# A hybrid HGRN2 and Conformer step on one core: norms whose intermediate values stand in PSUM, and a squared ReLU made by ACT in its PSUM bank

## The chip, the cores and the metric

The kernel runs on one core of a Trainium2 chip. The metric is the device time of one execution in microseconds. TensorE is called PE (its weight loads PEld), VectorE DVE, ScalarE ACT, GpSimd POOL and SyncE SP, as in the profile.

## What is computed

Two layers work on 640 tokens of 1024 features in float32: 128 context tokens and 512 latent tokens. Each layer has a mixer (layer 0 a bidirectional gated linear recurrence, layer 1 a convolution module) and a squared-ReLU MLP with 4096 hidden features. Ahead of each stands an RMS norm with a scale and a shift, which differ between context and latent tokens; the convolution module has a layer norm of its own, and a final norm ends the step. Cut to what matters here:

```python
y = xf * lax.rsqrt(jnp.mean(xf * xf, axis=-1, keepdims=True) + EPS)
hp = rmsnorm(xp, norm_mlp[i]) * (1.0 + m_ctx[4]) + m_ctx[3]
hs = rmsnorm(xs, norm_mlp[i]) * (1.0 + m_lat[4]) + m_lat[3]
return jnp.square(jax.nn.relu(h @ w1)) @ w2
# conformer_conv, after the depthwise convolution
uf = (uf - mu) * lax.rsqrt(var + EPS) * ln_g + ln_b
return jax.nn.silu(uf) @ w_pw2
```

## The kernel before, in words

**Layout and matmuls.** Features lie on the 128 partitions in eight tiles (k = 0 to 7), tokens on the free axis. Tokens go in two halves, A (tag "a", "c") and B ("b", "d"), of 320 and 320 columns, or in layer 1 after the convolution of 304 and 336 (COLS, L52). A half A holds context and latent columns, so that `segs` (L55) cuts it in two segments, 128 and 192 (or 176) columns; a half B is one segment. Each float32 operand is split in a rounded part `hi` and a rest `lo` (both fp32r): `split` (L168) has ACT copy the source to `hi` (L169) and DVE subtract it (L170). A unit of `linear` (L210) is one output tile of 128 features: eight k by three matmuls (L180, L183, L184), 24 in all, summed in one of the three PSUM banks of pool `mmp`, and then an evacuation function that is handed the bank.

**Weights.** `fetch` (L154) keeps three units ahead: a DMA to `rw`, ACT's rounding to `wh` (L161), and the rest `wl` (L165) made by DVE or, in a large part of the program (up to about 1300 us), by POOL in four pieces of 128x256.

**The order of the work.** The program is written as one stream. Background steps stand in the list `bg` with a cost each; after every unit `between` (L195) lets as many run as the budget pays for, and `drain` (L204) runs the rest. A scheduler in the framework then sorts each engine's instructions by the order of the program and its own estimate of when they are ready, hands out the buffers of each pool in turn, and adds the waits. Each engine then runs its own list strictly in order.

**Norms.** `rms_stat` (L246) squares each tile on ACT (to `nsq`, SBUF, L256) and sums on DVE (to `nacc`, L257). `inv_rms` (L226) has two forms. The usual one sums over partitions with a matmul of `ones` (ps_n, L230), takes the root on ACT into the SBUF tile `rs` (L232), and has DVE invert it in place (L233). The by-token form (the two norms ahead of layer 0's MLP, and half B of the final norm) works on a few columns (L238 to L240) and spreads the result by matmuls into the PSUM tile ps_n (L242). `norm_steps` (L272) then applies it tile by tile: DVE multiplies x by rs into `nt` (SBUF, two buffers, L278); `modulate` (L264) scales and shifts `nt` in place, segment by segment, on DVE for the four k in `on_dve` (L270) and on ACT for the others (L268); `split` makes hi and lo.

**The layer norm of the convolution.** The taps (L794) sum in two PSUM banks at a time of pool `scp` (three banks); `mean` (L815) sums with a matmul of `ones` (ps_mu, L817) and has ACT copy it, divided by D, to the SBUF tile `mu` (L819); `sub` (L822) subtracts it from the eight tiles of `yc`; then come `rms_stat`, a multiplication by rs (L828), ACT's Silu (L829), all in place in `yc`, and `split`.

**Hidden units of the MLP.** `hid_evac` (L699) takes a unit's bank `ps`: ACT makes the ReLU into the SBUF tile `hr` (L703), DVE multiplies it by ps (L704), which is the bank's last use, and `split` makes hi and lo of `hr`. There are 128 such units. The units of `mlp_out` and of the mixers' output projections are evacuated by `residual` (L284), one DVE instruction per segment (L287).

**Where the norms stand.** After the output projection of layer 0 the norms of both halves (L733), with the loads and DVE sums (L128, `scratch`) for layer 1's scales behind them; half A's norm of layer 1 (L842) beside `mlp_in` of B; the layer norm of half A and the norm of half B (L849 to L856) beside `pw2` and `pw1`; the layer norm of half B (ahead of L862); the norm ahead of half B's last MLP (L863); the final norm (L872).

Of the kernel before, what the change touches and what calls it, by code (L numbers as in the profile page):

```python
# [48 lines left out]
ND = (1, 3, 5, 7)  # L49
ND0 = (0, 2, 4, 6)  # L50
# [19 lines left out]
def hybrid_step(ctx: ExitStack, tc: tile.TileContext, xt, vec, pos, masks, ident_in, state, c_rows, w_mod0, w_modt,  # L70
# [18 lines left out]
    pool.memset(ones[:], 1.0)  # L89
    eps = const.tile([P, 2], F32, name="eps")  # L90
# [135 lines left out]
    def inv_rms(tp, acc, n, by_token):  # L226

        ps = axp.tile([P, 512], F32, tag="ax", name="ps_n")
        if not by_token:
            pe.matmul(ps[:, :n], ones[:], acc, start=True, stop=True)  # L230
            rs = tp.tile([P, HW], F32, tag="rs", name="rs")
            act.activation(rs[:, :n], ps[:, :n], AF.Sqrt, bias=eps[:, 0:1], scale=1.0 / D)  # L232
            dve.reciprocal(rs[:, :n], rs[:, :n])  # L233
            return rs[:, :n]
# [11 lines left out]
    def rms_stat(tp, xs, n, by_token=False):  # L246
# [3 lines left out]
        def sq(k):  # L250
# [3 lines left out]
            else:  # L254
                t = tp.tile([P, HW], F32, tag="nsq", name="nsq", bufs=2)
                act.activation(t[:, :n], xs(k), AF.Square)  # L256
                dve.tensor_tensor(box["acc"][:, :n], box["acc"][:, :n], t[:, :n], ALU.add)  # L257
# [6 lines left out]
    def modulate(t, layer, which, k, lo, hi, eng=act):  # L264
        for s, a, b in segs(lo, hi):
            r, sc, bi = t[:, a - lo:b - lo], amod[:, layer, which, k, s:s + 1], mvec(layer, 3 * which, k, s)
            if eng is act:
                act.activation(r, r, AF.Identity, bias=bi, scale=sc)  # L268
            else:
                eng.tensor_scalar(r, r, sc, bi, ALU.mult, ALU.add)  # L270

    def norm_steps(tp, x, layer, which, acts, lo, hi, by_token, on_dve):  # L272
# [3 lines left out]
        def apply(k):  # L276
            t = tp.tile([P, HW], F32, tag="nt", name="nt", bufs=2)
            dve.tensor_tensor(t[:, :n], x[:, k, lo:hi], box["rs"], ALU.mult)  # L278
            modulate(t, layer, which, k, lo, hi, dve if k in on_dve else act)
            split(t[:, :n], acts[k][0][:, :n], acts[k][1][:, :n])  # L280
# [26 lines left out]
    with tc.tile_pool(name="start", bufs=1) as st:  # L307
# [78 lines left out]
        def first_norm(k0, k1):  # L386
            for k in range(k0, k1):
                pin(dve.tensor_tensor(x0[:, k], x0[:, k], rs[:], ALU.mult), int(k > 4))
                modulate(x0[:, k], 0, 0, k, 0, NT, dve)
# [306 lines left out]
    rp = ctx.enter_context(tc.tile_pool(name="rp", bufs=2))  # L696


    def hid_evac(hid):  # L699
        def evac(u, half, lo, hi, ps):  # L700
            n = hi - lo
            r = rp.tile([P, HW], F32, tag="hr", name="hr")
            act.activation(r[:, :n], ps, AF.Relu)  # L703
            dve.tensor_tensor(r[:, :n], ps, r[:, :n], ALU.mult)  # L704
            split(r[:, :n], hid[half][u][0][:, :n], hid[half][u][1][:, :n])
# [12 lines left out]

    def start_norm(layer, which, half, cols, first=True, by_token=False, on_dve=ND):

# [248 lines left out]
```

## Time and profile before

| | |
|---|---|
| median of three runs | 1619.97 us (1619.37 to 1620.06) |
| the profiled execution, its own time | 1616.84 us |
| its span, first to last instruction | 1614.9 us |
| mean granted clock of PE | 0.989 |
| busy: PE, DVE, ACT, POOL | 98%, 77%, 47%, 43% |

The span is 1.9 us short of the execution's own time, and this execution is 3.1 us under the median. PE's clock column gives the granted clock as a share of 2.4 GHz; 0.5 is 1.2 GHz. A wait is an engine's idle time ahead of an instruction, put down to the instruction that came last. A matmul's duration is longer than the distance to the next one, since matmuls are pipelined: 172 of them with 320 columns start in 25 us, one every 145 ns.

### The profile page before, as it was taken

Reading aid. Unit: us, or ns where it says so; the run is one execution under the profiler, and the core shown is the slowest. Engines: PE = TensorE matmul, PEld = TensorE weight load, DVE = VectorE, ACT = ScalarE, POOL = GpSimd, SP = SyncE. Lnnn points to the kernel's source line nnn. Section 1 sums busy time; section 2 is a strip of 40 time slices with the busy share of each in tenths; the row PEclk is TensorE's granted clock in tenths of the full one; section 3 lists DMA queues with packets and bytes.
Section 4 is the critical chain, followed back from the end, with each engine's and each line's share of the span. In section 5 each row is a group of like instructions: output and inputs, shape, how many; then the busy total and the mean of one; then the engine's idle time right before and its main releaser. Section 6 shows DMA issues by size and latency. Waiting matters only on the chain.

```text
span 1614.9 us, 32111 instructions
## 1 busy us (share of the span) xinstructions
PE 1578.3 (98%) x12810; PEld 1536.0 (95%) x12810; DVE 1249.4 (77%) x2222; ACT 761.9 (47%) x1227; POOL 694.0 (43%) x863
## 2 busy tenths in 40 slices
PE   8999999999999999999999999999999899999997
PEld 6899999988899999999999999989999899999997
DVE  5788888878738998788789997899999686555544
ACT  3566666665446313344454334764344554334321
POOL 3100000000484765555978888789898710000000
PEclk7999999999999999999999999999999999999998
DMA  9333333333253556766544444345454344444401
GB/s 360 129 112 113 112 112 113 112 109 103 101 190 122 181 183 224 235 225 208 169 144 144 156 146 145 129 134 169 157 164 148 122 153 158 144 144 144 144 27 66
DMA packets 71302, 240.11 MB, mean 149 GB/s; under 512 B 7792, under 2 KB 14576, under 8 KB 70128
## 3 DMA queue, kind: packets, MB, share of 16 engines
q1 hardware_dynamic: 71152, 238.06, 44.4%
q8 instruction: 101, 1.65, 0.4%
q14 instruction: 49, 0.40, 0.1%
HBM read 234.36 MB, written 3.67 MB: 147 GB/s over the span
## 4 chain that ended last, share of the span: by engine, by line
PE 76%; DVE 17%; POOL 2%; ACT 2%; issue 2%; DMA 0%; SPq 0%; DVEq 0%; POOLq 0%; ACTq 0%
PE ps_mm L180 23%; PE ps_mm L184 22%; PE ps_mm L183 22%; DVE ps_cv L794 3%; POOL wl L165 2%; DVE scratch L128 2%; PE ps_sc L504 2%; DVE nt L278 1%; DVE nacc L257 1%; DVE cl L170 1%; PE ps_u L588 1%; DVE hr L704 1%; DVE nt L270 1%; DVE yc L822 1%; DVE al L170 1%
## 5 line engine op out<-in xcount | busy, mean ns | idle before, releaser
L165 POOL TENSOR_TENSOR wl<-rw,wh 128x256 fp32r<-128x256 f32 x808 | 668.8, 861 | 568.1 <-ACT wh L161 561.6
L161 ACT CAST wh<-rw 128x1024 fp32r<-128x1024 f32 x334 | 348.4, 1046 | 314.4 <-PE ps_mm L184 230.8
L180 PE MATMUL ps_mm<-bh,wh 128*128 128x320 f32 (+1 forms) x1000 | 317.8, 318 | 2.8 <-ACT nt L268 2.6
L180 PE MATMUL ps_mm<-ah,wh 128*128 128x320 f32 (+1 forms) x1000 | 311.6, 312 | 1.9 <-ACT ah L169 1.1
L183 PE MATMUL ps_mm<-bh,wl 128*128 128x320 f32 (+1 forms) x1000 | 311.4, 312 | 0.0
L184 PE MATMUL ps_mm<-bl,wh 128*128 128x320 f32 (+1 forms) x1000 | 310.8, 311 | 0.0
L184 PE MATMUL ps_mm<-al,wh 128*128 128x320 f32 (+1 forms) x1000 | 308.0, 308 | 1.7 <-DVE al L170 1.7
L183 PE MATMUL ps_mm<-ah,wl 128*128 128x320 f32 (+1 forms) x1000 | 308.0, 308 | 0.0
L794 DVE SCALAR_TENSOR_TENSOR ps_cv<-ub,vt,ps_cv 128x319 f32<-128x319 f32 (+1 forms) x464 | 228.7, 555 | 0.4
L165 DVE TENSOR_TENSOR wl<-rw,wh 128x1024 fp32r<-128x1024 f32 x132 | 168.7, 1280 | 39.6 <-ACT wh L161 39.6
L180 PEld LDWEIGHTS ps_mm<-ah,wh 128*128 128x128 f32 x1000 | 188.6, 189 | 7.3 <-issue 3.4
L180 PEld LDWEIGHTS ps_mm<-bh,wh 128*128 128x128 f32 x1000 | 188.0, 188 | 5.7 <-ACT nt L268 2.8
L183 PEld LDWEIGHTS ps_mm<-ah,wl 128*128 128x128 f32 x1000 | 188.5, 188 | 3.2 <-issue 2.6
L184 PEld LDWEIGHTS ps_mm<-al,wh 128*128 128x128 f32 x1000 | 188.6, 189 | 3.1 <-DVE al L170 2.2
L183 PEld LDWEIGHTS ps_mm<-bh,wl 128*128 128x128 f32 x1000 | 187.9, 188 | 0.5
L184 PEld LDWEIGHTS ps_mm<-bl,wh 128*128 128x128 f32 x1000 | 188.1, 188 | 0.1
L287 DVE SCALAR_TENSOR_TENSOR xr<-ps_mm,mod,xr 128x128 f32<-128x128 f32 (+2 forms) x240 | 97.8, 434 | 112.3 <-PE ps_mm L184 111.9
L180 PE MATMUL ps_mm<-ch,wh 128*128 128x320 f32 (+1 forms) x576 | 176.8, 307 | 4.4 <-ACT ch L169 2.3
L180 PE MATMUL ps_mm<-dh,wh 128*128 128x320 f32 (+1 forms) x576 | 180.7, 314 | 0.0
L184 PE MATMUL ps_mm<-dl,wh 128*128 128x320 f32 (+1 forms) x576 | 180.0, 313 | 0.0
L183 PE MATMUL ps_mm<-dh,wl 128*128 128x320 f32 (+1 forms) x576 | 179.7, 312 | 0.0
L184 PE MATMUL ps_mm<-cl,wh 128*128 128x320 f32 (+1 forms) x576 | 176.7, 307 | 1.8 <-DVE cl L170 1.8
(209 smaller groups left out, 2550.4 us busy)
## 6 DMA issues: line engine op xcount, KB each, us to landing
rw<-in_w_mlp SPq DMA_DIRECT2D x230, 512.0 KB, 3.4
wm<-in_w_modt SPq DMA_DIRECT2D x80, 512.0 KB, 4.2
rw<-in_w_pw SPq DMA_DIRECT2D x48, 512.0 KB, 3.3
rw<-in_w_in SPq DMA_DIRECT2D x40, 512.0 KB, 3.5
wmb<-in_w_mod SPq DMA_DIRECT2D x8, 1024.0 KB, 10.1
rw<-in_w_out SPq DMA_DIRECT2D x16, 512.0 KB, 3.4
x<-in_xt SPq DMA_DIRECT2D x8, 320.0 KB, 5.7
xr<-in_xt SPq DMA_DIRECT2D x8, 320.0 KB, 6.2
```

The costliest lines, as they stand in the source:

```text
L128: tc.keep_in_program_order(dve.scalar_tensor_tensor(scratch, box["w"][:], 1.0, cbs[:, s], ALU.mult, ALU.mult, accum_out=raw_m[:, i, s:s + 1]))
L161: act.copy(wh[:], rw[:])
L165: eng.tensor_tensor(wl[:, k:k + step], rw[:, k:k + step], wh[:, k:k + step].bitcast(F32), ALU.subtract)
L170: eng.tensor_tensor(lo, src, hi.bitcast(F32), ALU.subtract)
L180: first = pe.matmul(ps[:, :n], wh[:, k, :], hi[:, :n], start=k == 0, stop=False)
L183: pe.matmul(ps[:, :n], wl[:, k, :], hi[:, :n], start=False, stop=False)
L184: pe.matmul(ps[:, :n], wh[:, k, :], lo[:, :n], start=False, stop=k == KT - 1)
L257: dve.tensor_tensor(box["acc"][:, :n], box["acc"][:, :n], t[:, :n], ALU.add)
L270: eng.tensor_scalar(r, r, sc, bi, ALU.mult, ALU.add)
L287: dve.scalar_tensor_tensor(x[:, u, a:b], ps[:, a - lo:b - lo], mvec(layer, chunk, u, s), x[:, u, a:b], ALU.mult, ALU.add)
L504: pe.matmul(ps[r:r + w, t * w:(t + 1) * w], x[:, s0:s0 + w], y[:, t0:t0 + w], start=True, stop=True, tile_position=(0, r))
L794: dve.scalar_tensor_tensor(box[i][:, :m], u[:, j:j + m], w, box[i][:, :m], ALU.mult, ALU.add)
```

## The change

The norms' helper tiles move from SBUF to PSUM. `nsq`, `nt` and the layer norm's `lt` take banks of pool `scp` (three banks in turn); the root and its inverse are made in place in the bank ps_n, and the mean stays in ps_mu (the division by D moves into a second constant matrix `ones_d`). In `norm_steps` one DVE instruction per segment multiplies x by the scale and by rs; ACT adds the shift on its way to hi; a second DVE instruction adds the shift again and subtracts hi to give lo. In `hid_evac` ACT makes ReLU and square in place in the unit's bank, and `split` reads the bank. The pool `rp`, the tiles `rs`, `nt`, `nsq`, `mu` in SBUF and the choice `on_dve` go away. By instructions per tile: half A before, one DVE multiplication, one hi, one lo, and two segment instructions on DVE or ACT; after, four on DVE and two on ACT, of half the width on average. Half B before, DVE two or three and ACT two or one; after, DVE two and ACT one. Per hidden unit: before, DVE two and ACT two; after, DVE one and ACT three.

```diff
--- before.py
+++ after.py
@@ -46,8 +46,6 @@
 CUT = 304
 CA = 5
 TM0 = True
-ND = (1, 3, 5, 7)
-ND0 = (0, 2, 4, 6)
 CB = 6
 COLS = (((0, HALF), (HALF, NT)), ((0, CUT), (CUT, NT)))
 
@@ -87,6 +85,8 @@
     mask = const.tile([P, NMASK, SB], U8, name="mask")
     ones = const.tile([P, P], F32, name="ones")
     pool.memset(ones[:], 1.0)
+    ones_d = const.tile([P, P], F32, name="ones_d")
+    pool.memset(ones_d[:], 1.0 / D)
     eps = const.tile([P, 2], F32, name="eps")
     pool.memset(eps[:, 0:1], EPS)
     pool.memset(eps[:, 1:2], EPS * P)
@@ -228,10 +228,9 @@
         ps = axp.tile([P, 512], F32, tag="ax", name="ps_n")
         if not by_token:
             pe.matmul(ps[:, :n], ones[:], acc, start=True, stop=True)
-            rs = tp.tile([P, HW], F32, tag="rs", name="rs")
-            act.activation(rs[:, :n], ps[:, :n], AF.Sqrt, bias=eps[:, 0:1], scale=1.0 / D)
-            dve.reciprocal(rs[:, :n], rs[:, :n])
-            return rs[:, :n]
+            act.activation(ps[:, :n], ps[:, :n], AF.Sqrt, bias=eps[:, 0:1], scale=1.0 / D)
+            dve.reciprocal(ps[:, :n], ps[:, :n])
+            return ps[:, :n]
         c = n // 4
         rc = tp.tile([P, 4], F32, tag="rc", name="rc", bufs=2)
         for i in range(4):
@@ -252,32 +251,34 @@
                 box["acc"] = tp.tile([P, HW], F32, tag="nacc", name="nacc", bufs=2)
                 act.activation(box["acc"][:, :n], xs(0), AF.Square)
             else:
-                t = tp.tile([P, HW], F32, tag="nsq", name="nsq", bufs=2)
+                t = scp.tile([P, 512], F32, tag="sc", name="nsq")
                 act.activation(t[:, :n], xs(k), AF.Square)
-                dve.tensor_tensor(box["acc"][:, :n], box["acc"][:, :n], t[:, :n], ALU.add)
+                dve.tensor_tensor(box["acc"][:, :n], t[:, :n], box["acc"][:, :n], ALU.add)
 
         def fin():
             box["rs"] = inv_rms(tp, box["acc"][:, :n], n, by_token)
 
         return box, [(0.45, lambda k=k: sq(k)) for k in range(KT)] + [(0.3 if by_token else 2.1, fin)]
 
-    def modulate(t, layer, which, k, lo, hi, eng=act):
+    def modulate(t, layer, which, k, lo, hi):
         for s, a, b in segs(lo, hi):
             r, sc, bi = t[:, a - lo:b - lo], amod[:, layer, which, k, s:s + 1], mvec(layer, 3 * which, k, s)
-            if eng is act:
-                act.activation(r, r, AF.Identity, bias=bi, scale=sc)
-            else:
-                eng.tensor_scalar(r, r, sc, bi, ALU.mult, ALU.add)
-
-    def norm_steps(tp, x, layer, which, acts, lo, hi, by_token, on_dve):
+            dve.tensor_scalar(r, r, sc, bi, ALU.mult, ALU.add)
+
+    def norm_steps(tp, x, layer, which, acts, lo, hi, by_token):
         n = hi - lo
         box, steps = rms_stat(tp, lambda k: x[:, k, lo:hi], n, by_token)
 
         def apply(k):
-            t = tp.tile([P, HW], F32, tag="nt", name="nt", bufs=2)
-            dve.tensor_tensor(t[:, :n], x[:, k, lo:hi], box["rs"], ALU.mult)
-            modulate(t, layer, which, k, lo, hi, dve if k in on_dve else act)
-            split(t[:, :n], acts[k][0][:, :n], acts[k][1][:, :n])
+            t = scp.tile([P, 512], F32, tag="sc", name="nt")
+            for s, a, b in segs(lo, hi):
+                c = slice(a - lo, b - lo)
+                sh = mvec(layer, 3 * which, k, s)
+                dve.scalar_tensor_tensor(t[:, c], x[:, k, a:b], amod[:, layer, which, k, s:s + 1], box["rs"][:, c],
+                                         ALU.mult, ALU.mult)
+                act.activation(acts[k][0][:, c], t[:, c], AF.Identity, bias=sh)
+                dve.scalar_tensor_tensor(acts[k][1][:, c], t[:, c], sh, acts[k][0][:, c].bitcast(F32),
+                                         ALU.add, ALU.subtract)
 
         return steps + [(0.85, lambda k=k: apply(k)) for k in range(KT)]
 
@@ -386,7 +387,7 @@
         def first_norm(k0, k1):
             for k in range(k0, k1):
                 pin(dve.tensor_tensor(x0[:, k], x0[:, k], rs[:], ALU.mult), int(k > 4))
-                modulate(x0[:, k], 0, 0, k, 0, NT, dve)
+                modulate(x0[:, k], 0, 0, k, 0, NT)
                 for half, (lo, hi) in enumerate(COLS[0]):
                     split(x0[:, k, lo:hi], h[half][k][0][:, :HALF], h[half][k][1][:, :HALF], (dve, pool)[half])
 
@@ -693,16 +694,14 @@
 
     linear(4, h, g_last, both, 4, lambda: None, 4)
     oright.close()
-    rp = ctx.enter_context(tc.tile_pool(name="rp", bufs=2))
 
 
     def hid_evac(hid):
         def evac(u, half, lo, hi, ps):
             n = hi - lo
-            r = rp.tile([P, HW], F32, tag="hr", name="hr")
-            act.activation(r[:, :n], ps, AF.Relu)
-            dve.tensor_tensor(r[:, :n], ps, r[:, :n], ALU.mult)
-            split(r[:, :n], hid[half][u][0][:, :n], hid[half][u][1][:, :n])
+            act.activation(ps, ps, AF.Relu)
+            act.activation(ps, ps, AF.Square)
+            split(ps, hid[half][u][0][:, :n], hid[half][u][1][:, :n])
         return evac
 
     hid = {}
@@ -716,10 +715,10 @@
     def mlp_out(layer, cols, group=8, done=None):
         linear(8, hid, residual(xr, layer, 5), cols, group, done=done)
 
-    def start_norm(layer, which, half, cols, first=True, by_token=False, on_dve=ND):
+    def start_norm(layer, which, half, cols, first=True, by_token=False):
 
         h[half] = new_act("ab"[half])
-        steps = norm_steps(tp, xr, layer, which, h[half], *cols, by_token, on_dve)
+        steps = norm_steps(tp, xr, layer, which, h[half], *cols, by_token)
         bg[:] = steps + bg if first else bg + steps
         return steps[-1]
 
@@ -730,7 +729,7 @@
 
     budget[1] = 3.0
     for cols in (A0, B0):
-        linear(8, on, residual(xr, 0, 2), cols, done=lambda half: start_norm(0, 1, half, COLS[0][half], False, TM0, ND0))
+        linear(8, on, residual(xr, 0, 2), cols, done=lambda half: start_norm(0, 1, half, COLS[0][half], False, TM0))
     drain()
     with tc.tile_pool(name="wm1", bufs=1) as wmp:
         scratch = wmp.tile([P, D], F32, name="scratch")
@@ -814,9 +813,8 @@
 
         def mean():
             ps = axp.tile([P, 512], F32, tag="ax", name="ps_mu")
-            pe.matmul(ps[:, :n], ones[:], lnb["sum"][:, :n], start=True, stop=True)
-            lnb["mu"] = cv.tile([P, HW], F32, tag="mu", name="mu")
-            act.activation(lnb["mu"][:, :n], ps[:, :n], AF.Copy, scale=1.0 / D)
+            pe.matmul(ps[:, :n], ones_d[:], lnb["sum"][:, :n], start=True, stop=True)
+            lnb["mu"] = ps
 
         def sub(k):
             dve.tensor_tensor(lnb["y"][:, k, :n], lnb["y"][:, k, :n], lnb["mu"][:, :n], ALU.subtract)
@@ -824,8 +822,9 @@
         box, steps = rms_stat(tp, lambda k: lnb["y"][:, k, :n], n)
 
         def fin(k):
-            y = lnb["y"][:, k, :n]
-            dve.tensor_tensor(y, y, box["rs"], ALU.mult)
+            t = scp.tile([P, 512], F32, tag="sc", name="lt")
+            y = t[:, :n]
+            dve.tensor_tensor(y, lnb["y"][:, k, :n], box["rs"], ALU.mult)
             act.activation(y, y, AF.Silu, bias=v("ln_b")[:, k:k + 1], scale=v("ln_g")[:, k:k + 1])
             split(y, acts[k][0][:, :n], acts[k][1][:, :n])
 
```

## Rows read from the trace of the kernel before

**Rows 1.** The page's first part: busy time, share of the span, instructions of each engine.

```profile
PE 1578.3 (98%) x12810; PEld 1536.0 (95%) x12810; DVE 1249.4 (77%) x2222; ACT 761.9 (47%) x1227; POOL 694.0 (43%) x863
```

**Rows 2.** Waits of PE: total us, times, longest us.

```profile
PE ps_n L238 <- DVE nacc L257: 4.4, 2, 2.6
...
PE ps_n L230 <- DVE nacc L257: 2.8, 2, 1.7
PE ps_mm L180 <- ACT nt L268: 2.6, 1, 2.6
PE ps_mm L180 <- ACT ch L169: 2.3, 1, 2.3
...
PE ps_mm L180 <- DVE xr L287: 2.1, 2, 1.3
...
PE ps_mm L184 <- DVE cl L170: 1.8, 5, 0.9
PE ps_mm L184 <- DVE al L170: 1.7, 2, 1.2
PE ps_mm L180 <- ACT ah L169: 1.1, 1, 1.1
```

**Rows 3.** Windows of 25 us: busy us (instructions) by engine, PEclk, DMA share, GB/s.

```profile
500.00:525.00 25.00, 22.43 (x149) 22.16 (x148) 18.97 (x42) 14.12 (x29) 9.76 (x12) 0.93 0.32 106
...
800.00:825.00 25.00, 22.25 (x138) 21.26 (x137) 22.05 (x37) 17.38 (x33) 17.25 (x23) 0.93 0.38 126
825.00:850.00 25.00, 25.00 (x173) 25.00 (x172) 22.24 (x50) 9.22 (x15) 22.88 (x33) 1.00 0.49 159
...
1050.00:1075.00 25.00, 21.56 (x144) 20.77 (x144) 21.62 (x39) 18.63 (x28) 22.66 (x29) 1.00 0.45 149
```

**Rows 4.** DVE lines from 400 to 1300 us: min/median/max ns.

```profile
L257 DVE TENSOR_TENSOR nacc<-nacc,nsq x51: 466/758/7968, 451.3 to 1300.0; 128x320 f32<-128x320 f32 x28, 128x304 f32<-128x304 f32 x14, 128x336 f32<-128x336 f32 x9
...
L278 DVE TENSOR_TENSOR nt<-xr,rs x24: 465/624/1024, 804.1 to 1087.0; 128x320 f32<-128x320 f32 x16, 128x304 f32<-128x304 f32 x8
...
L822 DVE TENSOR_TENSOR yc<-yc,mu x16: 460/1006/1048, 1000.2 to 1252.9; 128x304 f32<-128x304 f32 x8, 128x336 f32<-128x336 f32 x8
...
L170 DVE TENSOR_TENSOR dl<-hr,dh x32: 493/748/1043, 529.4 to 997.1; 128x320 fp32r<-128x320 f32 x32
...
L704 DVE TENSOR_TENSOR hr<-ps_mm,hr x88: 460/480/494, 508.5 to 1253.8; 128x320 f32<-128x320 f32 x64, 128x304 f32<-128x304 f32 x24
```

**Rows 5.** The same line of DVE after 1300 us, where POOL has no work.

```profile
L170 DVE TENSOR_TENSOR dl<-hr,dh x32: 500/501/502, 1343.4 to 1548.9; 128x336 fp32r<-128x336 f32 x32
```

**Rows 6.** DVE groups by shape: busy us, mean ns, idle before.

```profile
L287 DVE SCALAR_TENSOR_TENSOR xr<-ps_mm,mod,xr 128x128 f32<-128x128 f32 x80 | 27.8, 347 | 53.0 <-PE ps_mm L184 52.9
...
L287 DVE SCALAR_TENSOR_TENSOR xr<-ps_mm,mod,xr 128x192 f32<-128x192 f32 x40 | 16.3, 407 | 0.0
...
L287 DVE SCALAR_TENSOR_TENSOR xr<-ps_mm,mod,xr 128x320 f32<-128x320 f32 x40 | 21.8, 544 | 11.9 <-PE ps_mm L184 11.7
...
L270 DVE TENSOR_SCALAR nt<-nt,amod,mod 128x320 f32<-128x320 f32 x8 | 4.5, 560 | 0.0
...
L233 DVE RECIPROCAL rs<-rs 128x320 f32<-128x320 f32 x2 | 4.3, 2146 | 3.7 <-ACT rs L232 3.7
```

**Rows 7.** ACT groups by shape: busy us, mean ns, idle before.

```profile
L703 ACT ACTIVATE hr<-ps_mm 128x320 f32<-128x320 f32 x64 | 27.9, 436 | 86.0 <-PE ps_mm L184 86.0
...
L161 ACT CAST wh<-rw 128x1024 fp32r<-128x1024 f32 x334 | 348.4, 1046 | 314.4 <-PE ps_mm L184 230.8 <-POOL wl L165 69.2 <-DMA rw<-in_w_pw 5.4
```

**Rows 8.** Timeline of DVE around 1250 us, then ACT: start us, us.

```profile
1249.98 3.91 DVE L822 TENSOR_TENSOR yc<-yc,mu 128x336 f32<-128x336 f32 x4
...
1253.81 0.46 DVE L704 TENSOR_TENSOR hr<-ps_mm,hr 128x304 f32<-128x304 f32 x1
...
1254.31 0.45 ACT L169 CAST ch<-hr 128x304 fp32r<-128x304 f32 x1 [3.25 <-DVE hr L704]
```

**Rows 9.** Timeline at the end of the program, PE.

```profile
1604.82 0.76 PE L238 MATMUL ps_n<-ones,nacc 128*84 128x1 f32 x8 [1.78 <-DVE nacc L257]
```

## The prediction

> **What bounds the kernel now.** I read the page's busy times first: PE is busy for 1578.3 us of the span of 1614.9 [rows 1], so what can be won is the 36.6 us in which it idles, and what a low clock takes from it. Nothing in the change touches a unit's 24 matmuls. The waits of PE come next [rows 2]: almost all that are over a microsecond stand at norms, and they end on DVE (the sum nacc, the residual xr, the rest al or cl) or on an ACT step that itself stood behind DVE (nt, ch). The windows show how large the holes are: a full stretch starts 173 matmuls in 25 us, the stretch of layer 1's first norm 138, and there the granted clock is 0.93 on average [rows 3]. So has the stretch of layer 0's norms [rows 3]. A clock that is at 2.4 GHz or at 1.2 was then at 1.2 for 0.07 x 25 / 0.5 = 3.5 us, which costs at most 1.75 us beside the waits themselves.
>
> Why DVE is late is seen in its own lines. Instructions with both inputs in SBUF have medians of 624 to 1006 ns while POOL makes weight rests, and maxima over 1000; the one that reads a PSUM bank beside the same POOL work has 480, and never over 494 [rows 4]. After 1300 us, where POOL rests, the slow line costs 501 [rows 5]. So a PSUM operand takes DVE out of POOL's way. The change gives nearly every DVE instruction of the norms one PSUM operand, and that is the main term.
>
> **The change, part by part.** The two-input forms that are new (multiply by scale and rs; add the shift, subtract hi) are nearest to the residual, which has one PSUM and one SBUF tensor and a scalar: 347, 407 and 544 ns for 128, 192 and 320 columns [rows 6]. A sum, subtraction or multiplication with a PSUM operand I price at 0.48, the hi-lo subtraction of a hidden unit too. As far ends I keep 0.46, the fastest of these lines, and 1.05, the slowest [rows 4], by which nothing would be won.
>
> *A tile of a norm* costs DVE before 0.62 (multiply), 0.28 (half of the tiles modulated at 0.56, taken as one piece) and 0.75 (lo, as for a hidden unit): 1.65 [rows 4, 6]. After, a half A has two segments: 2 x (0.347 + 0.407) = 1.51. A half B: 2 x 0.544 = 1.09. A sum of squares goes from 0.76 to 0.48, a mean's subtraction from 1.01 to 0.48, a hidden unit from 0.48 + 0.75 to 0.48. What this is worth is read place by place, never more than the wait there:
>
> 1. Norms of layer 0's MLP. Wait 2.6 (of the 4.4 on L238 the other 1.8 is the final norm [rows 2, 9]), with up to 1.75 of low clock. Their rs is in PSUM already, so a tile of half A goes from 1.51 to 1.51; seven sums save 7 x 0.28 = 1.9. I take 1.8 of 4.3.
> 2. Layer 1's first norm, half A. Waits on al and ah 1.7 + 1.1, low clock 1.75: 4.5; the window agrees, 35 matmuls short at 145 ns, 5.1 [rows 2, 3]. DVE saves 8 x 0.14 + 5 hidden units x 0.75 = 4.8. PE wants tile 7 only 21 x 0.145 = 3.0 us after tile 0 and DVE needs 1.5 us a tile, so a remnant stays: 3.5.
> 3. Layer norm, half A: wait 1.7 on L230. Eight subtractions and seven sums save 4.2 + 1.9, and the copy of the mean goes: all 1.7.
> 4. Norms beside pw1 of half B: 2.6 on nt and 0.8 on xr. DVE saves 8 x (1.65 - 1.09) + 6 x 0.28 = 6.2, but the next norm's sums compete: 2.9 of 3.4 (the window is 29 matmuls short, 4.2, with the room that the norm's own matmul takes [rows 3]).
> 5. Layer norm, half B: ch 2.3, cl 0.9, nacc 1.1 (2.8 less 1.7). The timeline shows the cause: four subtractions hold DVE for 3.91 us, the squared ReLU's multiplication stands behind them, and hi waits 3.25 us for it [rows 8]. After, hi needs ACT alone. The chain from the last subtraction to the sum stays: 3.0 of 4.3.
> 6. Layer 0's MLP beside the scale loads: xr 1.3 and four small waits on cl, 0.9. DVE stays full of those loads' sums: 1.4 of 2.2.
>
> Sum 14.3; all the waits together 20.4. The end of the program (1.8 us on nacc [rows 9]) keeps its chain residual, square, sum, and POOL rests there: nothing. The extra constant of the mean is one POOL memset behind the one that PE waits for: nothing.
>
> *What is added.* ACT makes 128 more squares of about 0.436 us [rows 7], 56 us in a program in which it is busy for 762 [rows 1]; the idle 53% hides them; its part of a norm's tile stays at one or two instructions. A bank is held for ReLU, square, hi and lo, 3 x 0.44 + 0.48 = 1.8, with one weight rounding of 1.05 between them 2.9, where before it was 0.9; PE wants that bank again two units later, 2 x 24 x 0.145 = 7.0, so 4.1 us cover it. At a change from mlp_in to mlp_out in one half (12 places) the cover is thinner: hi of the last tile is ready 3 x 0.44 + 1.05 = 2.4 after the unit, and PE wants it at 3.05. A second rounding in between makes it 3.45, 0.4 late: up to 4.8 us in all, in the range and not in the sum. Behind the waiting ACT stands the next rounding, whose weights are wanted three units later.
>
> *The reciprocal in PSUM* is shown by no row of this trace. From SBUF it takes 2.15 for 320 columns [rows 6]. At the other end it takes double, and four of them (places 2 to 5) lie ahead of a wait: 8.6. Below, it could gain only the hundredths by which PSUM and undisturbed SBUF differ. I take 2.15: at 6.7 ns a column it is nearly four times slower than the multiply-add from SBUF at 1.75, so it isn't the reading that bounds it. The Trainium skill, VectorE: DVE Perf Modes, section Why PSUM operands drop a tier, says that an instruction with a PSUM operand can't use both SBUF read ports, and that fp32 then runs at its single rate. By that rule the double price is the one to fear, and the sum would be 14.3 - 8.6 = 5.7.
>
> The profiled execution takes 1616.84, its span and 1.9 around it; 14.3 less is 1602.5. It lies 3.1 under the median of the runs, so against that median, 1619.97, the forecast is 1605.7. A difference of 0.2% (3.2 us) is what a measurement of this kernel can tell.
>
> **The rivals.**
> *Partly given back.* The phase changes cost their 4.8, or one or two reciprocals their double: 9 us stay, 1611. For it: ACT's list is strictly in order. Against: ACT is idle for long stretches.
> *DVE and ACT take turns at a bank.* In a half A the second segment's multiplication goes to the bank that ACT reads for the first, and each lo waits for its hi. If DVE waited each of these out, a tile would take 1.51 + 2 x 0.44 = 2.4, 0.75 more than the 1.65. Places 1 and 2 turn to +6.0 - 1.9 = 4.1 and +6.0 - 3.7 = 2.3 lost, the other four keep 9.0: 2.6 won, 1617.4, no change that can be told. Against: three banks in turn let other tiles fill the gaps. The Trainium skill, PSUM — Partial Sum Buffer, section PSUM bank collisions raise a hardware error, says that two engines may not be in one bank and quadrant at once, reads included. By it the turns are forced, and only the filling is open.
> *PE's own list* (slower). The sum's matmul stands at a fixed place in PE's list, set from estimates when the program is built, and blocks every unit behind it. Two of the three largest entries of [rows 2] are that. If the estimates for the new forms are too short, each of ten such matmuls (two by token, six norms, two means) waits like the worst now, 2.6: 26 in place of 5.4, while places 2, 4, 6 and the ch of 5 still win 9.8: 10.8 slower, 1630.8. It decides from 1.5 us per matmul on. Against: DVE's work ahead of each sum gets shorter whatever the list says.
> *Nothing arrives.* The waits move to other instructions of the same places: 1619.
>
> **How the numbers follow.** Forecast 0.58, partly given back 0.20, turns 0.08, nothing arrives 0.05, PE's list 0.09. Faster 0.78, within 0.2% 0.13, slower 0.09. The time is the likeliest case's, 1605.7. The range runs from all waits gone, 1619.97 - 20.4 = 1599.6, to the turns at 1617.4; it leaves out the slower case, the empty one and a little at the ends.
>
> **What would show it.** Right: the sums, subtractions and multiplications of the norms near 0.48 us also beside POOL; DVE's busy time down by 75 us or more (128 x 0.6 for the hidden units alone); full windows at the norms; PE's waits on nt, ch, ah and xr under 2 us together. Wrong: a reciprocal of 4 us; PE waits on ps_n or ps_mu longer than now; new waits on hi or lo at the changes from mlp_in to mlp_out; or DVE idle behind ACT inside a norm of half A.

## The result and the profile after

The changed kernel takes 1594.13 us (median of four runs, 1593.40 to 1595.34) beside 1619.67 for the kernel before on the same chip (four runs, 1618.63 to 1620.06): ratio 0.9845 [0.9833, 0.9857], 25.5 us or 1.6% faster. Forecast were 1605.7 and a range from 1599.6: the sign was right and the gain nearly twice as large as forecast, 5.5 us beyond the near end of the range.

The profiled execution after takes 1594.12 us, its span 1592.3. First its page, busy time and chain of work:

```profile
PE 1572.4 (99%) x12810; PEld 1532.4 (96%) x12810; DVE 1127.9 (71%) x2106; ACT 797.9 (50%) x1341; POOL 662.3 (42%) x864
...
PE 87%; DVE 5%; POOL 2%; ACT 2%; issue 2%; DMA 1%; SPq 0%; DVEq 0%; POOLq 0%; ACTq 0%
```

Against [rows 1] PE idles for 19.9 us in place of 36.6, DVE works 121.5 us less, and ACT only 36 more. The waits of PE after (total us, times, longest us):

```profile
PE ps_s L372 <- DVE acc L334: 3.3, 1, 3.3
PE ps_rb L683 <- DVE o_all L685: 2.2, 2, 1.2
PE ps_n L237 <- DVE nacc L256: 1.7, 1, 1.7
...
PE ps_mm L180 <- ACT ah L279: 1.3, 2, 0.8
...
PE ps_mm L184 <- DVE bl L280: 0.9, 1, 0.9
```

Of the norms' waits [rows 2] 1.3 on ah, 0.9 on bl and the 1.7 at the end of the program [rows 9] are left. The two largest entries belong to layer 0's recurrence and to its output heads, which the change doesn't touch. DVE's lines from 400 to 1300 us (min/median/max ns), the same work as in [rows 4]:

```profile
L256 DVE TENSOR_TENSOR nacc<-nsq,nacc x56: 464/492/509, 450.5 to 1291.8; 128x320 f32<-128x320 f32 x28, 128x304 f32<-128x304 f32 x14, 128x336 f32<-128x336 f32 x14
...
L820 DVE TENSOR_TENSOR yc<-yc,ps_mu x16: 464/484/504, 990.0 to 1231.4; 128x304 f32<-128x304 f32 x8, 128x336 f32<-128x336 f32 x8
...
L827 DVE TENSOR_TENSOR lt<-yc,ps_n x16: 466/488/511, 1005.9 to 1252.2; 128x304 f32<-128x304 f32 x8, 128x336 f32<-128x336 f32 x8
...
L170 DVE TENSOR_TENSOR dl<-ps_mm,dh x32: 473/492/494, 524.7 to 988.2; 128x320 fp32r<-128x320 f32 x32
```

Medians of 748 to 1006 ns and maxima over 1000 (once 7968) have become 484 to 492 with no instruction over 511, beside a POOL that does the same work as before (808 subtractions). The layer norm's multiplication `lt`, not among [rows 4], had a median of 880 and a maximum of 1046. By shape (busy us, mean ns, idle before) the new forms stand so:

```profile
L277 DVE SCALAR_TENSOR_TENSOR nt<-xr,amod,ps_n 128x128 f32<-128x128 f32 x24 | 8.4, 350 | 1.5 <-PE ps_n L241 1.4
...
L277 DVE SCALAR_TENSOR_TENSOR nt<-xr,amod,ps_n 128x192 f32<-128x192 f32 x16 | 6.7, 420 | 0.4
...
L280 DVE SCALAR_TENSOR_TENSOR al<-nt,mod,ah 128x192 fp32r<-128x192 f32 x16 | 6.7, 417 | 4.3 <-ACT ah L279 4.2
...
L232 DVE RECIPROCAL ps_n<-ps_n 128x320 f32<-128x320 f32 x2 | 4.3, 2167 | 5.2 <-ACT ps_n L231 5.2
...
L702 ACT ACTIVATE ps_mm<-ps_mm 128x320 f32<-128x320 f32 x64 | 27.0, 422 | 86.8 <-PE ps_mm L184 86.7
...
L703 ACT ACTIVATE ps_mm<-ps_mm 128x320 f32<-128x320 f32 x64 | 27.6, 431 | 0.2
```

The prices 347 and 407 from [rows 6] and ACT's 436 [rows 7] were good to some 3%.

**Where the time came from.** The same matmuls are followed through both traces: a window of the kernel before, and the window of the kernel after that starts and ends with the same units. Columns: length, PE busy (matmuls started), clock, DMA share, GB/s. Before:

```profile
500.00:531.00 31.00, 28.43 (x189) 0.94 0.31 102
531.00:780.00 249.00, 246.21 (x1670) 1.00 0.63 214
803.10:826.10 23.00, 20.25 (x125) 0.93 0.34 115
1005.10:1045.10 40.00, 38.32 (x267) 1.00 0.37 121
1045.00:1075.00 30.00, 26.46 (x178) 1.00 0.46 153
1240.00:1290.00 50.00, 44.97 (x309) 1.00 0.38 126
```

After:

```profile
499.20:529.00 29.80, 28.00 (x189) 1.00 0.28 89
529.00:774.40 245.40, 245.40 (x1671) 1.00 0.63 217
797.40:816.70 19.30, 18.65 (x125) 1.00 0.37 125
995.80:1033.80 38.00, 38.00 (x266) 1.00 0.43 144
1033.80:1059.30 25.50, 25.50 (x178) 1.00 0.44 145
1223.80:1267.90 44.10, 44.10 (x309) 1.00 0.47 155
```

In the order of the program these are places 1, 6, 2, 3, 4 and 5 of the forecast: 1.2, 3.6, 3.7, 2.0, 4.5 and 5.9 us shorter, 20.9 of the 22.6 us between the spans. Of the other 1.7, 0.8 stands ahead of 500 us, where nothing is changed; there two profiles of the kernel before differ by more (the second, below, is 1.8 us ahead of the first at 45 us). In four of the six places PE now never idles, and the two stretches of low clock are gone.

### The profile page after: what moved, and what is told of

It reads as the page before. It is cut to its first block, busy times and chain, and to the rows that moved or that the text cites. A ratio compares the mean times of both kernels' runs of the same rounds, so it can differ in the third digit from the quotient of the medians.

```text
span 1592.3 us, 32135 instructions
## 1 busy us (share of the span) xinstructions
PE 1572.4 (99%) x12810; PEld 1532.4 (96%) x12810; DVE 1127.9 (71%) x2106; ACT 797.9 (50%) x1341; POOL 662.3 (42%) x864
## 4 chain that ended last, share of the span: by engine, by line
PE 87%; DVE 5%; POOL 2%; ACT 2%; issue 2%; DMA 1%; SPq 0%; DVEq 0%; POOLq 0%; ACTq 0%
PE ps_mm L180 27%; PE ps_mm L184 26%; PE ps_mm L183 26%; POOL wl L165 2%; PE ps_sc L505 2%; DMA rw<-in_w_in 1%; PE ps_u L589 1%; DVE scr L128 1%; ACT xy L515 1%; PE ps_m L350 1%; DVE a L521 0%; PE ssq L461 0%; DVE a L523 0%; PE ps_o L604 0%; DVE al L280 0%
## 5 line engine op out<-in xcount | busy, mean ns | idle before, releaser
L165 POOL TENSOR_TENSOR wl<-rw,wh 128x256 fp32r<-128x256 f32 x808 | 637.2, 823 | 577.1 <-ACT wh L161 576.8
L793 DVE SCALAR_TENSOR_TENSOR ps_cv<-ub,vt,ps_cv 128x319 f32<-128x319 f32 (+1 forms) x464 | 224.1, 558 | 0.1
```

Of the source, the lines that this page charges most:

```text
L165: eng.tensor_tensor(wl[:, k:k + step], rw[:, k:k + step], wh[:, k:k + step].bitcast(F32), ALU.subtract)
L793: dve.scalar_tensor_tensor(box[i][:, :m], u[:, j:j + m], w, box[i][:, :m], ALU.mult, ALU.add)
```

## The experiments

The theory of the forecast (A): DVE instructions with two inputs in SBUF are held up by POOL's weight rests, and one operand in PSUM takes them out of POOL's way. Against it stand that fewer and merged instructions do it, that ACT's share does it, and that the banks or the schedule do it.

### Half of the change alone

*The hidden units alone*, in the kernel before:

```diff
-            r = rp.tile([P, HW], F32, tag="hr", name="hr")
-            act.activation(r[:, :n], ps, AF.Relu)
-            dve.tensor_tensor(r[:, :n], ps, r[:, :n], ALU.mult)
-            split(r[:, :n], hid[half][u][0][:, :n], hid[half][u][1][:, :n])
+            act.activation(ps, ps, AF.Relu)
+            act.activation(ps, ps, AF.Square)
+            split(ps, hid[half][u][0][:, :n], hid[half][u][1][:, :n])
```

> The kernel before with the new evacuation of hidden units alone; norms as before. Theory A (the norms' PSUM operands bring most): 6 to 9 us faster than before, about 1611 to 1614, from the stretch of the scale loads (3.8 us in the changed kernel's trace) and a part of the two places where hidden units stand among norm steps. Theory B (the hidden units' shorter chain brings most): 13 us or more, 1607 or less, and DVE busy about 95 us less.

Measured: 1612.71 us (1605.56 to 1615.64, ten runs), ratio 0.9956 [0.9942, 0.9969], 7 us faster. At place 6 PE never idles in this kernel (its window, columns as above), and between the same matmuls it is 3.7 us shorter than before, as much as in the changed kernel:

```profile
531.00:780.00 249.00, 249.00 (x1695) 1.00 0.61 214
```

The norms' lines kept a slow part; DVE's sum and multiplication:

```profile
L257 DVE TENSOR_TENSOR nacc<-nacc,nsq x51: 462/629/7832, 451.5 to 1299.7; 128x320 f32<-128x320 f32 x28, 128x304 f32<-128x304 f32 x14, 128x336 f32<-128x336 f32 x9
...
L278 DVE TENSOR_TENSOR nt<-xr,rs x24: 463/518/5282, 804.1 to 1088.8; 128x320 f32<-128x320 f32 x16, 128x304 f32<-128x304 f32 x8
```

*The norms alone*: the changed kernel with the hidden units of the kernel before (the diff above, read the other way).

> The changed kernel with the hidden units evacuated as before (ReLU to SBUF on ACT, multiplication on DVE). Theory A: 15 to 18 us faster than before, 1602 to 1605. Theory B: 10 us or less, 1610 or more. If the two parts simply add, this run's gain and that of the run with hidden units alone make 25 us.

Measured: 1599.52 us (1598.00 to 1601.31), ratio 0.9881 [0.9866, 0.9896], 20 us faster, more than theory A gave it. The halves add up: 7 + 20 = 27 beside 25.5 for both. Here places 2, 3 and 4 give 3.8, 2.0 and 4.5 us, as in the changed kernel, and place 6 only 0.4: place 6 belongs to the hidden units, the other three to the norms.

### The placement taken back, and the placement alone

*The new instructions with their tiles in SBUF* (the norms; `nsq`, the mean and `lt` likewise):

```diff
-            act.activation(ps[:, :n], ps[:, :n], AF.Sqrt, bias=eps[:, 0:1], scale=1.0 / D)
-            dve.reciprocal(ps[:, :n], ps[:, :n])
+            rs = tp.tile([P, HW], F32, tag="rs", name="rs")
+            act.activation(rs[:, :n], ps[:, :n], AF.Sqrt, bias=eps[:, 0:1], scale=1.0 / D)
+            dve.reciprocal(rs[:, :n], rs[:, :n])
...
-            t = scp.tile([P, 512], F32, tag="sc", name="nt")
+            t = tp.tile([P, HW], F32, tag="nt", name="nt", bufs=2)
```

> The changed kernel with the same new instructions in the norms, but their helper tiles (squares, applied tile, inverse root, mean, the layer norm's product) in SBUF; hidden units stay in PSUM. Theory A (the place of the operand counts, since a DVE instruction with two SBUF inputs is held up by POOL): the norms' DVE lines go back to means of 600 ns and more beside POOL, and 8 to 13 us of the gain are lost, 1602 to 1607. Theory C (fewer and shorter instructions count, not the place): within 3 us of the changed kernel, 1591 to 1597.

Measured: 1614.71 us (1610.55 to 1615.51, ten runs), ratio 0.9964 [0.9954, 0.9974]: of the 25.5 us won, 20.6 are lost again. The norms' lines in this kernel, 400 to 1300 us:

```profile
L257 DVE TENSOR_TENSOR nacc<-nsq,nacc x52: 458/636/7801, 452.0 to 1299.4; 128x320 f32<-128x320 f32 x28, 128x304 f32<-128x304 f32 x14, 128x336 f32<-128x336 f32 x10
...
L278 DVE SCALAR_TENSOR_TENSOR nt<-xr,amod,rs x40: 333/474/4270, 800.2 to 1084.9; 128x128 f32<-128x128 f32 x16, 128x192 f32<-128x192 f32 x8, 128x320 f32<-128x320 f32 x8, 128x176 f32<-128x176 f32 x8
...
L822 DVE TENSOR_TENSOR yc<-yc,mu x16: 460/901/1045, 998.2 to 1247.1; 128x304 f32<-128x304 f32 x8, 128x336 f32<-128x336 f32 x8
```

The loss has theory A's sign and is larger than its 8 to 13 us. This kernel stands 2 us above the one with the hidden units alone, so the merged instructions by themselves win nothing.

*The old instructions with their tiles in PSUM* (the kernel before, hidden units as they were; `nsq` and the layer norm's tile in `scp`, root, inverse and mean in their banks):

```diff
-            t = tp.tile([P, HW], F32, tag="nt", name="nt", bufs=2)
+            t = scp.tile([P, 512], F32, tag="sc", name="nt")
             dve.tensor_tensor(t[:, :n], x[:, k, lo:hi], box["rs"], ALU.mult)
```

> The kernel before with its own instructions in the norms (multiply, modulate on DVE or ACT, split) and its own hidden units, but the norms' helper tiles in PSUM as in the changed kernel (squares, applied tile, inverse root, mean, the layer norm's product). Theory A (the operand's place alone): near the run with all of the norms' change, 1599.5, so 1599 to 1603. Theory E (place and fusion are both needed, since lo, the modulation and the multiplication stay three instructions): 1605 to 1611.

Measured: 1599.94 us (1598.45 to 1600.96), ratio 0.9853 [0.9808, 0.9898], in a job (a set of kernels timed together) in which the kernel before took 1620.77 (1615.35 to 1630.35, seven runs). That is the time of the norms alone, 1599.52, without one merged instruction. Two of its DVE lines:

```profile
L258 DVE TENSOR_TENSOR nacc<-nacc,nsq x56: 459/486/505, 451.5 to 1297.9; 128x320 f32<-128x320 f32 x28, 128x304 f32<-128x304 f32 x14, 128x336 f32<-128x336 f32 x14
...
L822 DVE TENSOR_TENSOR yc<-yc,ps_mu x16: 465/484/503, 995.2 to 1243.8; 128x304 f32<-128x304 f32 x8, 128x336 f32<-128x336 f32 x8
```

The norms' part of the gain is the placement, all of it as far as these times tell.

### The hidden units' squares by ACT, but in SBUF

```diff
-            act.activation(ps, ps, AF.Relu)
-            act.activation(ps, ps, AF.Square)
-            split(ps, hid[half][u][0][:, :n], hid[half][u][1][:, :n])
+            r = rp.tile([P, HW], F32, tag="hr", name="hr")
+            act.activation(r[:, :n], ps, AF.Relu)
+            act.activation(r[:, :n], r[:, :n], AF.Square)
+            split(r[:, :n], hid[half][u][0][:, :n], hid[half][u][1][:, :n])
```

> The changed kernel with ACT still making ReLU and square, but in an SBUF tile that hi and lo are made from. Theory A: lo has two SBUF inputs again and costs 0.6 to 0.75 us beside POOL in place of 0.48; 2 to 5 us slower than the changed kernel, 1596 to 1599. Theory D (only that the multiplication left DVE counts): within 1.5 us of the changed kernel.

Measured: 1598.52 us (1597.61 to 1600.38), ratio 0.9876 [0.9861, 0.9891], 4.4 us above the changed kernel. The hi-lo subtraction has its slow form back:

```profile
L170 DVE TENSOR_TENSOR dl<-hr,dh x32: 491/880/1022, 524.3 to 988.4; 128x320 fp32r<-128x320 f32 x32
```

With the norms in PSUM, the hidden units' part of the change is worth 5.4 us (1599.52 less 1594.13). 4.4 of it go when the squares stand in SBUF, though ACT still makes them: here too it is mostly the place and hardly the engine.

### POOL's reads taken away

Three kernels in which POOL writes zeros to the weight rests in place of subtracting: that of the new instructions in SBUF, the changed one, and the one before. All three leave out POOL's weight rests from the 41st weight tile on, so the matmuls with these rests multiply by zeros, and POOL's pieces are shorter (a median of 312 ns in place of 741). The first zeros are written at 391 to 396 us.

```diff
-                eng.tensor_tensor(wl[:, k:k + step], rw[:, k:k + step], wh[:, k:k + step].bitcast(F32), ALU.subtract)
+                if eng is pool and i >= 40:
+                    pool.memset(wl[:, k:k + step].bitcast(F32), 0.0)
+                else:
+                    eng.tensor_tensor(wl[:, k:k + step], rw[:, k:k + step], wh[:, k:k + step].bitcast(F32), ALU.subtract)
```

> The run with the new norms in SBUF, and POOL's subtractions for the rests of the weights (from the 41st weight tile on) replaced by writing zeros to the same tiles: those rests are left out of the matmuls, and POOL no longer reads SBUF. Theory A (POOL's reading holds up DVE's two-input instructions): the norms' DVE lines fall to about 500 ns and the time comes to that of the changed kernel, 1590 to 1597, though every helper tile stays in SBUF. Theory F (tiles in SBUF are slow for another reason, such as two buffers in place of three): the time stays above 1608.

> The changed kernel with the same rests of the weights left out, POOL writing zeros instead. Theory A: its DVE lines of the norms are out of POOL's way already, so it gains 3 us at most, 1591 to 1594. If POOL slows the changed kernel in another way (the scale loads' sums have two SBUF inputs), more.

> The kernel before with the same rests of the weights left out, POOL writing zeros instead. Theory A: most of the gain appears without any change of the norms, 1596 to 1603; what is left to the changed kernel is the shorter work of DVE. Theory F: 1613 or more.

Measured: new instructions in SBUF 1585.96 us (1584.92 to 1587.88), ratio 0.9770 [0.9717, 0.9824]; changed kernel 1590.37 (1588.98 to 1590.74), 0.9793 [0.9749, 0.9837]; kernel before 1586.43 (1586.08 to 1589.32), 0.9774 [0.9730, 0.9819]. The same edit is worth 34 us to the kernel before (1620.77 in that job), 29 to the new instructions in SBUF (1614.71), and 4 to the changed kernel; the last two compare different jobs, and in the first the runs of the kernel before lie 15 us apart. The new instructions in SBUF came 4 us below the 1590 that theory A gave as their least, the changed kernel 0.6 below its range; theory F, that tiles in SBUF are slow for another reason, is out. Of the kernel before with the silent POOL, the page and two DVE lines with both inputs in SBUF (its lines are numbered three on):

```profile
PE 1567.3 (99%) x12810; PEld 1530.6 (97%) x12810; DVE 1157.3 (73%) x2222; ACT 759.6 (48%) x1227; POOL 248.9 (16%) x863
```

```profile
L281 DVE TENSOR_TENSOR nt<-xr,rs x28: 461/484/504, 791.1 to 1298.2; 128x320 f32<-128x320 f32 x16, 128x304 f32<-128x304 f32 x8, 128x336 f32<-128x336 f32 x4
...
L825 DVE TENSOR_TENSOR yc<-yc,mu x16: 466/486/510, 982.7 to 1224.9; 128x304 f32<-128x304 f32 x8, 128x336 f32<-128x336 f32 x8
```

The same 2222 DVE instructions take 92 us less [rows 1], the subtraction of the mean goes from 1006 to 486 ns [rows 4], and nothing was moved to PSUM. And it wins at the same places: between the same matmuls of the two traces places 1, 6, 2, 3, 4 and 5 are 4.2, 4.0, 4.7, 1.9, 4.5 and 5.4 us shorter. So what held DVE was POOL's reading, and what the change wins is the escape from it. The zeros aren't the cause: the changed kernel has them too and gains 4. Nor is it only that POOL works for less time: between 400 and 1300 us, 19 instructions of the norms and hidden units with both inputs in SBUF ran wholly beside POOL's writing, and none took over 510 ns. The Trainium skill, SBUF — State Buffer, section SBUF: two separate sides, states that DVE and GpSimd share one pair of ports under an exclusive lock, which a DVE instruction with two SBUF inputs needs only against a GpSimd instruction that reads SBUF. The three kernels agree: a POOL that works on the same tiles but only writes leaves DVE at 0.48.

I had expected the kernel before to come to 1596 to 1603 here. It came to 1586, 4 us below the changed kernel with the same edit: where POOL reads nothing, PSUM buys nothing. Of these 4 us, 3.2 are there already at 40 us, before any changed step (the same matmul of PE starts at 40.2 and 36.9 us; at 36.0 in the new instructions in SBUF) and 350 us before POOL's first zeros; why, no run shows, but two profiles of the same kernel before differ there by 1.8 us. Behind that the two kernels differ by 1.0 us. The changed one has two waits of PE there that neither SBUF kernel has:

```profile
PE ps_mm L187 <- DVE bl L283: 0.9, 1, 0.9
...
PE ps_mm L183 <- ACT ah L282: 0.5, 1, 0.5
```

### The kernel before once more, and one step further

The third job ran the kernel before as it was, for a second profile, the changed kernel as it was, and a kernel that goes one step further: layer 0's output heads are multiplied in place in the PSUM bank.

```diff
-        ps = axp.tile([P, 512], F32, tag="ax", name="ps_rb")
+        pl, tg = ((scp, "sc"), (axp, "ax"))[i % 3 == 2]
+        ps = pl.tile([P, 512], F32, tag=tg, name="ps_rb")
...
-        dve.tensor_tensor(o, ps[:, :HALF], o, ALU.mult)
-        split(o, on[half][i][0][:, :HALF], on[half][i][1][:, :HALF])
+        dve.tensor_tensor(ps[:, :HALF], ps[:, :HALF], o, ALU.mult)
+        split(ps[:, :HALF], on[half][i][0][:, :HALF], on[half][i][1][:, :HALF])
```

> The kernel before, unchanged, profiled once more. What it tells apart is where 2.8 us of the gain came from that the profiled pair of executions does not show: the traced gain is 22.7 us, the gain of the medians 25.5. Theory A: the profiled execution of before was a short one, since it had only two stretches at 1.2 GHz in the middle of the program (at 506 and 814 us), and another execution of the same kernel has more or longer ones: here three or more, or longer than 3.4 us, and a time of 1618 to 1622. Rival: the difference lies in no stretch of low clock; then this trace has the same two, of the same length, and yet a time of 1618 to 1622.

Measured: 1621.70 us, 4.9 above the profiled execution that the forecast started from. Its windows between 50 and 1600 us where the clock isn't 1.00 (columns as above):

```profile
500.00:525.00 25.00, 22.42 (x128) 0.80 0.31 106
1050.00:1075.00 25.00, 21.79 (x136) 0.93 0.40 126
1250.00:1275.00 25.00, 22.16 (x136) 0.86 0.32 106
```

Theory A of this run holds: three stretches at 1.2 GHz, each in a window in which PE had waited, some 20 us together ((0.20 + 0.07 + 0.14) x 25 / 0.5), where the first profile had two in [rows 3], 7 us. Behind 45 us it is 6.5 us longer than the first profile, and the same matmuls lie 3.1, 2.8 and 0.9 us further apart around these three stretches (places 1, 4 and 5). 13.5 us more at half the clock cost up to 6.7. The kernel's times differ from run to run by as much: 1615.34 to 1623.38 over the nine runs of this job, the shortest with a mean clock of 0.989, the others with 0.986 or 0.987.

> The changed kernel, unchanged, beside the two others of this job, so that the kernel with the heads treated alike has its own partner on the same chip: 1593 to 1596, 24 to 27 us under the kernel before.

Measured: 1594.46 us (1593.40 to 1595.42, five runs), ratio 0.9845 [0.9831, 0.9859].

> The changed kernel, with one more step of the same kind: layer 0's output heads are multiplied in place in the PSUM bank that spread the reciprocal root (pools sc and ax in turn) and split from there, so that DVE's subtraction there has a PSUM operand. Theory A (what counts is that DVE reads no second input from SBUF beside POOL): the two waits of the matmul behind o_all, 2.2 us together in the changed kernel, shrink to under 0.8, and the kernel is 1 to 3 us faster than the changed one. Rival (the wait there is the length of the chain of one head, matmul, root, reciprocal, spreading matmul, and not DVE's reads): the waits stay near 2, the time is within 0.7 us of the changed kernel's.

Measured: 1591.33 us (1588.81 to 1591.85), ratio 0.9823 [0.9808, 0.9838]: 3.1 us under its partner, no run of the one within the runs of the other. The window of the heads in the partner, then in this kernel, and its subtraction:

```profile
405.00:455.00 50.00, 47.36 (x286) 1.00 0.36 128
```

```profile
405.00:455.00 50.00, 50.00 (x312) 1.00 0.41 143
...
L170 DVE TENSOR_TENSOR cl<-ps_rb,ch x8: 423/478/493, 411.6 to 423.1; 128x320 fp32r<-128x320 f32 x8
```

The waits behind o_all are gone. By itself this leaves the rival (the length of the chain) open, since the kernel also takes three more banks for these tiles. The changed kernel with the silent POOL settles it: its heads keep their banks and their chain, and there is no wait on o_all in it either. Its window:

```profile
405.00:455.00 50.00, 50.00 (x305) 1.00 0.39 137
```

Between 45 and 500 us it gains 3.4 us on the changed kernel of this job, and the step further 3.8, so most of it is POOL's reading. The step further is the fastest kernel here that computes everything.

## Why the prediction was right in its mechanism and wrong in its size

**Right.** POOL holds up DVE's instructions with two inputs in SBUF, and a PSUM operand frees them: sums, subtractions and multiplications came to 0.48 to 0.49, as priced. DVE's busy time fell by 121.5 us (75 or more forecast), and the waits on nt, ch, ah and xr went from 8.1 [rows 2] to 1.3. Places 2 and 3 came to 3.7 and 2.0, forecast 3.5 and 1.7. ACT's work stayed hidden, at the changes from mlp_in to mlp_out no wait on hi or lo came up, and the end of the program kept its 1.7 us.

**The reciprocal in PSUM** takes 2167 ns where it took 2146 [rows 6]; the near end was right. The rule that was weighed against it (the Trainium skill, VectorE: DVE Perf Modes, Why PSUM operands drop a tier) doubles nothing here.

**Wrong, first: the takes.** The step that failed is "never more than the wait there", with the remnants left at places 4, 5 and 6. Forecast was 14.3 for the six places, measured 20.9 (and 1.7 elsewhere): place 4 gave 4.5 and not 2.9 of 3.4, place 5 gave 5.9 and not 3.0 of 4.3, place 6 gave 3.6 and not 1.4 of 2.2. Only place 1 gave less, 1.2 and not 1.8, since waits on ah and bl of 0.8 and 0.9 came up there. There were two errors. The first: the remnants. The competition that was to leave remnants at 4 and 5 (the next norm's sums, the chain to the sum) was itself made of the slow form: when all of DVE's list gets faster, it gets out of its own way too. At 6 it was not. The scale loads' sums keep both inputs in SBUF and stay slow, before and then after:

```profile
L128 DVE SCALAR_TENSOR_TENSOR scratch<-wm,cbs 128x1024 f32<-128x1024 f32 x96 | 134.7, 1403 | 3.3 <-DMA wm<-in_w_modt 3.0
```

```profile
L128 DVE SCALAR_TENSOR_TENSOR scratch<-wm,cbs 128x1024 f32<-128x1024 f32 x96 | 129.9, 1353 | 14.4 <-DMA wm<-in_w_modt 14.1
```

What made room there is the hidden units' shorter work: DVE is busy for 181.9 us of place 6 in place of 211.9. The second error: a wait isn't the time that it costs. The six windows before hold 18.4 us of PE's idle time and those after 2.5, 15.9 less, and yet they are 20.9 shorter. At most 3.5 of the difference is the low clock (0.06 x 31 + 0.07 x 23). The others are matmuls that PE starts late or slowly around a wait without being shown as idle, as in the timeline of the kernel before (start us, us, and in brackets the idle time):

```profile
566.19 0.30 PE L184 MATMUL ps_mm<-cl,wh 128*128 128x320 f32 x1
567.29 0.41 PE L180 MATMUL ps_mm<-ch,wh 128*128 128x320 f32 x1 [0.80 <-DVE hr L704]
567.54 0.30 PE L183 MATMUL ps_mm<-ch,wl 128*128 128x320 f32 x1
567.69 0.31 PE L184 MATMUL ps_mm<-cl,wh 128*128 128x320 f32 x1
```

From one start to the next it is 1.10 and then 0.25 us, in place of 0.145 each: 1.06 lost, 0.80 shown. This wait (place 6), and one of 0.7 on the layer norm's sum `lsum` (place 5), were also missing from the list of places. So was the wait on o_all at layer 0's heads, 1.9 us before: "almost all that are over a microsecond stand at norms" passed over it, and the step further shows that it has the same cause. So "all waits gone", 1599.6, was no end of the range, but lay above the result.

**Wrong, second: the offset.** The forecast set the sum against the median and so added 3.1 us that the profiled execution had been below it. The changed kernel's profiled execution lies on its median (1594.12 and 1594.13). Other executions of the kernel before have stretches of low clock that this profile had not, as the second profile shows; that the 3.1 us are such stretches fits, but the runs behind the median have no profile. The change takes away the waits, and with them these stretches are gone: after has none between 50 and 1575 us. Without the offset the forecast would have been 1602.5, and the miss 8.4 us, not 11.6.

**The rivals.** Partly given back, turns at a bank and nothing arrives gave a smaller gain or none, PE's own list a loss, and none of them came. One sign of being wrong did appear: DVE waits for ACT inside a norm's tile of half A, each lo for its hi, 4.2 us over the 16 instructions of 192 columns in the rows after and 7.8 over all 48. PE sees little of it, no wait on al and 1.3 us on ah, and a turn at the bank hardly shows: the 16 multiplications of the second segment came after 0.4 us of idle time in all. The sums' matmuls of PE's list, feared for ten waits, have lost the waits they had, save the last norm's.

**Left open.** Why the changed kernel is 3 to 4 us behind the SBUF kernels at 40 us when POOL is silent; and why place 1 gives only 1.2 us with the change but 4.2 to the kernel before with the silent POOL: two waits of 1.8 us together remain there, and the rest isn't traced.

## What to carry to other kernels

When DVE's simple instructions with two inputs in SBUF have medians well over their fastest case, look at whether POOL reads SBUF at the same time; if it does, give them one operand in PSUM, or give POOL work that doesn't read. Placement is the lever, not the count of instructions: it was worth 20 us here with the old instructions, and the new ones without it won nothing. When a change takes away a cause that all of an engine's list shares, price PE's gain by the distance between the starts of the same matmuls, not by the idle time shown, and don't let each place keep a remnant.

## What the runs showed of the hardware that was not expected

- POOL's reading cost DVE 92 us of busy time in the kernel before (1249.4 to 1157.3, the same instructions). To the program the edit was worth 34 us by the medians of its job, and 27 between the same matmuls behind 45 us in the two profiles. POOL seems to lose too: its median subtraction takes 741 ns before and 742 after, but its mean falls from 861 to 823 once DVE's operands stand in PSUM.
- A DVE instruction can be shut out until POOL's row of work ends. One sum of 128x336 took 7.8 to 8.0 us in three kernels with its operands in SBUF (maxima of nacc above and in [rows 4]), each time where POOL worked through a long row of rests. The timeline of the kernel before, DVE and then the part of POOL's row from 1280 us on (start us, us):

```profile
1291.00 7.97 DVE L257 TENSOR_TENSOR nacc<-nacc,nsq 128x336 f32<-128x336 f32 x1 [1.03 <-ACT nsq L256]
1300.00 0.51 DVE L257 TENSOR_TENSOR nacc<-nacc,nsq 128x336 f32<-128x336 f32 x1 [0.55 <-ACT nsq L256]
```

```profile
1279.78 18.83 POOL L165 TENSOR_TENSOR wl<-rw,wh 128x256 fp32r<-128x256 f32 x27
```

  POOL's row ends at 1298.61 and the sum at 1298.97, 0.36 later, where its next like takes 0.51. With the hidden units alone changed and with the norms in SBUF the sum also ends 0.36 us after POOL's row. Most instructions beside such rows take about 1 us at most, as the four of [rows 8]; why this one waited until eleven of POOL's subtractions were through, no run shows. The forecast's far end, "1.05, the slowest [rows 4]", passed over the 7968 in the first of those rows.
- In a kernel without POOL's reads, one operand in PSUM buys nothing: 1590.4 us beside 1586.0 and 1586.4, most of the difference from ahead of any changed step.
- How much of an execution of the kernel before ran at 1.2 GHz differed between executions, 7 and 20 us in two profiles, each time in windows in which PE had waited. The changed kernel, at 1593.4 to 1595.4 in nine runs, has both less of the waits and less of the spread.
